# A two-layer diffusion backbone on one core: the opening of the first layer in a written-out order on all five engines

## Chip, core and metric

The kernel runs on one core of a Trainium2 chip. The time is the device time of one execution in microseconds (us). The core's engines work beside each other and wait for each other through semaphores: TensorE (PE in the profile, its weight loads PEld), VectorE (DVE), ScalarE (ACT), GpSimd (POOL), and SyncE (SP), which here only issues DMAs.

## The reference, cut to what matters

Two layers over 512 latent tokens (`x`) and 256 context tokens (`ctx`) of width 1024. The part of a layer that the change touches is its beginning: the modulation vectors, the norm, and the projection by `w_in`.

```python
mod_lat = jnp.split(jax.nn.silu(c) @ w_mod[layer] + b_mod[layer], MOD_CHUNKS, axis=-1)
mod_ctx = jnp.split(jax.nn.silu(c_ctx) @ w_mod[layer] + b_mod[layer], MOD_CHUNKS, axis=-1)
sh1, sc1, g1, sh2, sc2, g2 = [m[:, None, :] for m in mod_lat]
csh1, csc1, cg1, csh2, csc2, cg2 = mod_ctx
h_lat = rms_norm(x, attn_pre_norm[layer]) * (1 + sc1) + sh1
h_ctx = rms_norm(ctx, attn_pre_norm[layer]) * (1 + csc1) + csh1
...
(a_q, a_k, a_v, a_r, a_z, ...) = split_cols(h_lat @ w_in)
```

Behind it come three token mixers (gated linear attention, banded attention, global attention), an output projection and a gated ConvFFN, none of which the change touches.

## The kernel before

`start()` is the opening of layer 0. The 768 tokens are six tiles of 128: `tiles = (4, 5, 0, 1, 2, 3)`, the two context tiles first; I call them t0 to t5 in this order. The width of 1024 is eight k-tiles of 128 (`KT`).

- **Norm and turn of a tile.** `norm()`: ScalarE squares the tile and sums the squares (L561); `rsqrt1` makes the inverse root from the sum in five small steps (VectorE L260, ScalarE L261, VectorE L264 to L266); VectorE scales the tile by it (L563); TensorE transposes it in eight pieces into PSUM (L565), called the *turn* here; ScalarE copies k-tiles 0 to 3 and VectorE k-tiles 4 to 7 to `xt` (L566, L567).
- **Modulation.** `mod(h)`, h = 0, 1, multiplies the two vectors `c` and `c_ctx` by a half of the shift and scale columns of `w_mod`: half h serves k-tiles 4h to 4h + 3. For each half there are eight loads of 512 KB (L531), k0 to k7, and in four *pairs* of k 16 matmuls with a moving size of 512 (L535). The trace counts each fp32 matmul as two.
- **Sums and application.** `apply(h)` first adds the bias to the product (VectorE L541), turns it to columns on TensorE (L544) and writes shift and scale (L546, L547). Then, for context columns 512 to 767 and latent columns 0 to 255 and 256 to 511, and four k-tiles each: ScalarE writes the modulated value rounded to fp32r (hi, L552), VectorE scales the full value in place (L553), and VectorE, for odd k GpSimd, subtracts the two (lo, L554).
- **First projection.** `half(h, tiles)` multiplies four k-tiles of a token tile by 288 columns of `w_in` (512 to 799): 12 matmuls (L490 to L492), hi times hi, lo times hi, hi times lo. The weights are split in the same way (`weight`, L479 on ScalarE, L480 on VectorE or GpSimd). After half 1 of a tile, `rz_out` takes the result out (L696 to L699).

What sets the order: a scheduler orders the instructions of an engine by their estimated readiness, except on engines that stand in a `manual_schedule`. There they keep the order in which the code is written. In `start()` SP's order is written by hand throughout, `weave` mixing the six norms with the four pairs of `mod(0)`; TensorE's is written by hand from the first `half` on, by the table `HALF`, which puts pairs of `mod(1)` between the halves; ScalarE's and VectorE's for the second application alone. `columns()` loads four small arrays (L302 to L305), behind the second context tile in SP's program by the table entry `XF`, and turns them to columns.

Of the kernel before, what the change touches and what calls it, by code (L numbers as in the profile page):

```python
# [27 lines left out]
XF = 1  # L28
# [179 lines left out]
class Kernel:  # L208
# [90 lines left out]
    def columns(self, raw):  # L299

# [4 lines left out]
        nc.sync.dma_start(raw.f[16:32], io["ffn_pre_norm"].rearrange("l (k p) -> (l k) p", p=P))  # L305
        ps = self.mring.next()
# [159 lines left out]
    def weight(self, src, kt, w, lo="v"):  # L466
# [8 lines left out]
        else:  # L475
            nc.sync.dma_start(rv, src.rearrange("(k p) n -> p k n", p=P))
# [18 lines left out]
    def start(self, X):  # L495
# [8 lines left out]
        tring = PRing(self.PS, [(0, 2), (2, 2), (4, 2)])  # L504
        tiles = (4, 5, 0, 1, 2, 3)
        rows = F.alloc(P)
        xl = {}
        for t in tiles:
            xl[t] = xs.next().f
            nc.sync.dma_start(xl[t], self.xin(t))  # L510
            if t == tiles[XF]:
                self.columns(rows)
        sel = F.alloc(2, 2)
        idv = self.ident.rearrange("p (x j q) -> p x j q", x=2, j=2)
        nc.vector.tensor_tensor(sel.f, idv[:, 0, :, 0:2], idv[:, 1, :, 0:2], ALU.add)
# [3 lines left out]
        acc = {}  # L519
        for h in range(2):  # L520
            nc.vector.memset(ms[h].f, 0.0)
            for r in range(2):
                nc.sync.dma_start(ms[h].f[r:64:32], bm[h])

        def mod(h):

            acc[h] = ps = self.PS[:, (6 + h) * 512:(7 + h) * 512]
            for k in range(0, KT, 2):
                ws = [raw.next().f, raw.next().f]
                for x in range(2):  # L530
                    nc.sync.dma_start(ws[x], wm[h, (k + x) * P:(k + x + 1) * P])  # L531
                for x in range(2):
                    for j in range(2):
                        g = 32 * (2 * x + j)
                        nc.tensor.matmul(ps[g:g + 32, :], self.cT[:, k + x, :], ws[x][:, j], start=(k == 0), stop=(k == KT - 2), tile_position=(0, g))  # L535
                yield

        def apply(h):
# [9 lines left out]
            yield  # L548
            for r, a, b in ((1, 512, 768), (0, 0, 256), (0, 256, 512)):
                for k in range(4 * h, 4 * h + 4):  # L550
                    s, o = A[:, r, k:k + 1], B[:, r, k:k + 1]
                    nc.scalar.activation(X.r[:, 0, k, a:b], xt.f[:, k, a:b], AF.Identity, bias=o, scale=s)  # L552
                    nc.vector.tensor_scalar(xt.f[:, k, a:b], xt.f[:, k, a:b], s, o, ALU.mult, ALU.add)  # L553
                    (nc.gpsimd if k % 2 else nc.vector).tensor_tensor(X.r[:, 1, k, a:b], xt.f[:, k, a:b], X.f[:, 0, k, a:b], ALU.subtract)  # L554

        def norm():
            for t in tiles:
                x = xl[t]
# [1024 lines left out]
```

## Time and profile before

| | us |
|---|---|
| median of three runs | 1786.04 |
| lowest, highest | 1784.34, 1786.31 |
| profiled execution, device time | 1782.25 |
| its span in the trace | 1780.2 |
| TensorE busy in it | 1715.3 (96%) |
| VectorE, ScalarE, GpSimd busy | 1157.4, 794.9, 540.8 |

The opening is about the first 60 us of the span. In the page's row of 40 slices (44.5 us each) TensorE's first slice reads 7 tenths, and nearly all others 9 or 8; the DMA engines' first slice reads 9. The chain of work that ended last is TensorE's by 74%. A row of a timeline gives the start, the duration, the engine, the line and the operation, and in square brackets how long the engine had been idle and who released it.

### The profile page before, as it was taken

How to read it: one execution, taken by the hardware profiler on the slowest of the kernel's cores; microseconds unless marked ns; L12 is line 12 of the kernel's file. 1: busy time of each engine (PE TensorE's matmuls, PEld its weight loads, DVE VectorE, ACT ScalarE, POOL GpSimd, SP SyncE). 2: the span in 40 equal slices, each digit the busy share in tenths (PEclk: the TensorE clock that was granted, in tenths of full speed). 3: DMA queues.
4: the chain of work that ended last, by engine and by line, in shares of the span. 5: the costliest groups of instructions: out<-in, count | busy, mean ns of one | idle time of the engine just before them, and what ended most of it. 6: DMA issues, size and time to landing. Idle time of an engine off the chain costs nothing.

```text
span 1780.2 us, 29135 instructions
## 1 busy us (share of the span) xinstructions
PE 1715.3 (96%) x11226; PEld 1448.8 (81%) x11226; DVE 1157.4 (65%) x2356; ACT 794.9 (45%) x1652; POOL 540.8 (30%) x485
## 2 busy tenths in 40 slices
PE   7999989999899999999999999998999999999997
PEld 4898876779898888878888878878778988888886
DVE  5548986663868799774755584499764754555544
ACT  5635446773643313122221355453774653333322
POOL 2325454440420202122020262345542222222223
PEclk9999999999999999999999999999999999999999
DMA  9311134112433334353432342111105443333202
GB/s 316 92 45 37 61 101 140 58 49 94 158 117 109 112 117 153 104 182 91 152 119 71 111 144 68 49 37 49 36 1 154 149 136 95 107 95 93 73 30 89
DMA packets 169038, 177.77 MB, mean 100 GB/s; under 512 B 7382, under 2 KB 137640, under 8 KB 168644
## 3 DMA queue, kind: packets, MB, share of 16 engines
q1 hardware_dynamic: 168612, 173.56, 30.8%
q0 software_dynamic: 288, 2.36, 0.4%
q8 instruction: 88, 1.44, 0.3%
q14 instruction: 50, 0.41, 0.1%
HBM read 165.38 MB, written 10.51 MB: 99 GB/s over the span
## 4 chain that ended last, share of the span: by engine, by line
PE 74%; DVE 15%; DMA 4%; issue 4%; ACT 3%; POOL 0%; SPq 0%; DVEq 0%; ACTq 0%; POOLq 0%
PE psum L1344 28%; PE psum L490 10%; PE psum L491 10%; PE psum L492 10%; PE psum L1113 4%; PE psum L1090 3%; DMA arena_f<-in_w_mod 3%; DVE arena_f L425 2%; PE psum L1063 2%; DVE arena_r L480 2%; PE psum L1064 1%; DVE arena_f L1201 1%; DVE arena_f L1075 1%; PE psum L366 1%; PE psum L1046 1%
## 5 line engine op out<-in xcount | busy, mean ns | idle before, releaser
L1344 PE MATMUL psum<-zone_Z,arena_r 128*128 128x256 f32 (+1 forms) x2760 | 516.0, 343 | 5.2 <-DVE arena_f L1351 3.0
L1344 PEld LDWEIGHTS psum<-zone_Z,arena_r 128*128 128x128 f32 x2760 | 435.8, 189 | 74.9 <-issue 3.8
L490 PE MATMUL psum<-arena_r,zone_Z 128*128 128x256 f32 (+2 forms) x1124 | 343.9, 307 | 5.7 <-ACT arena_f L1273 3.8
L491 PE MATMUL psum<-arena_r,zone_Z 128*128 128x256 f32 (+2 forms) x1124 | 343.3, 306 | 2.7 <-POOL zone_Z L635 2.2
L492 PE MATMUL psum<-arena_r,zone_Z 128*128 128x256 f32 (+2 forms) x1124 | 342.3, 306 | 0.0
L490 PEld LDWEIGHTS psum<-arena_r,zone_Z 128*128 128x128 f32 x1124 | 213.9, 191 | 22.9 <-issue 7.6
L491 PEld LDWEIGHTS psum<-arena_r,zone_Z 128*128 128x128 f32 x1124 | 214.3, 191 | 16.6 <-issue 3.7
L492 PEld LDWEIGHTS psum<-arena_r,zone_Z 128*128 128x128 f32 x1124 | 214.0, 191 | 12.8 <-issue 4.4
L480 DVE TENSOR_TENSOR arena_r<-arena_f,arena_r 128x1024 fp32r<-128x1024 f32 (+1 forms) x111 | 157.5, 1422 | 89.7 <-ACT arena_r L479 86.2
L479 ACT CAST arena_r<-arena_f 128x1024 fp32r<-128x1024 f32 (+1 forms) x114 | 118.8, 1049 | 145.3 <-PE psum L1344 106.3
L425 DVE SCALAR_TENSOR_TENSOR arena_f<-arena_f 128x256 f32<-128x256 f32 (+1 forms) x224 | 138.9, 657 | 36.1 <-DMA arena_f<-in_w_mod 35.6
L1355 POOL TENSOR_TENSOR arena_f<-arena_f 128x768 f32<-128x768 f32 (+1 forms) x44 | 75.6, 1717 | 277.7 <-DVE arena_f L1351 250.9
L1408 DVE TENSOR_TENSOR arena_f<-arena_f,psum 128x512 f32<-128x512 f32 x100 | 68.0, 683 | 103.6 <-PE psum L492 103.5
L1334 POOL TENSOR_TENSOR arena_r<-arena_f,arena_r 128x1024 fp32r<-128x1024 f32 x22 | 53.9, 2450 | 264.3 <-ACT arena_r L1333 264.3
L1078 POOL TENSOR_SCALAR arena_f<-arena_f 128x768 f32<-128x768 f32 (+3 forms) x96 | 79.3, 829 | 89.5 <-DVE arena_f L1077 72.5
L1334 POOL TENSOR_TENSOR zone_Z<-arena_f,zone_Z 128x1024 fp32r<-128x1024 f32 x22 | 53.9, 2448 | 161.8 <-ACT zone_Z L1333 161.7
L1075 DVE TENSOR_REDUCE arena_f<-psum 128x1 f32<-128x768 f32 (+4 forms) x120 | 90.9, 766 | 14.1 <-PE psum L1064 12.1
L1349 ACT ACTIVATE arena_f<-psum,arena_f 128x512 f32<-128x512 f32 (+1 forms) x132 | 89.0, 701 | 24.1 <-PE psum L1344 24.1
L1350 DVE SCALAR_TENSOR_TENSOR arena_f<-psum,arena_f 128x511 f32<-128x511 f32 (+1 forms) x132 | 84.0, 651 | 20.0 <-ACT arena_f L1349 20.0
L1344 PE MATMUL psum<-zone_Z 128*128 128x512 f32 (+1 forms) x408 | 86.9, 366 | 0.7 <-POOL zone_Z L635 0.6
L1354 ACT ACTIVATE arena_f<-arena_f 128x768 f32<-128x768 f32 (+1 forms) x44 | 32.5, 739 | 119.1 <-DVE arena_f L1351 119.1
L1351 DVE SCALAR_TENSOR_TENSOR arena_f<-psum,arena_f 128x511 f32<-128x511 f32 (+1 forms) x132 | 84.7, 654 | 1.4
(291 smaller groups left out, 3120.2 us busy)
## 6 DMA issues: line engine op xcount, KB each, us to landing
arena_f<-in_ffn_w_up SPq DMA_DIRECT2D x88, 512.0 KB
arena_f<-in_w_mod SPq DMA_DIRECT2D x112, 256.0 KB
arena_f<-in_ffn_w_down SPq DMA_DIRECT2D x44, 512.0 KB
arena_f<-in_w_in SPq DMA_DIRECT2D x24, 512.0 KB
zone_Z<-in_w_mod SPq DMA_DIRECT2D x48, 256.0 KB
arena_f<-in_w_out SPq DMA_DIRECT2D x16, 512.0 KB
xd<-arena_f SPq DMA_DIRECT2D x16, 512.0 KB
arena_f<-xd SPq DMA_DIRECT2D x14, 512.0 KB
```

The lines of the kernel that those rows point to most:

```text
L425: nc.vector.scalar_tensor_tensor(av[:, r], x[:, i], s, av[:, r], ALU.mult, ALU.add)
L479: nc.scalar.copy(hr, rv)
L480: (nc.vector if lo == "v" else nc.gpsimd).tensor_tensor(lr, rv, hf, ALU.subtract)
L490: mm(out, lh, rh, start=first, stop=False)
L491: mm(out, ll, rh, start=False, stop=False)
L492: mm(out, lh, rl, start=False, stop=last)
L1075: nc.vector.tensor_reduce(st[:, 0:1], ps[:, 0:w], AX.X, ALU.max, negate=True)
L1334: nc.gpsimd.tensor_tensor(wp.r[:, 1], rd.f, wp.f[:, 0], ALU.subtract)
L1344: nc.tensor.matmul(p[:, po:po + n], us[s][wi][:, k], X.r[:, xi, k, o:o + n], start=(k == 0 and (wi, xi) == (0, 0)), stop=(k == KT - 1 and ...
L1349: nc.scalar.activation(d, p, AF.Identity, bias=ci[:, 3:4], scale=ci[:, 1:2])
L1350: nc.vector.scalar_tensor_tensor(d[:, 1:n], p[:, 0:n - 1], ci[:, 0:1], d[:, 1:n], ALU.mult, ALU.add)
L1351: nc.vector.scalar_tensor_tensor(d[:, 0:n - 1], p[:, 1:n], ci[:, 2:3], d[:, 0:n - 1], ALU.mult, ALU.add)
```

## The change

All of the opening is now written out in one `manual_schedule` of the five engines.

- SP: the four small arrays first (`load_columns`), then the context tiles, w_mod k0 to k3 of the first half, the first half of the `w_in` columns, k4 and k5, the bias of the first half, k6 and k7, the latent tiles, and the second half's w_mod, bias and `w_in`.
- TensorE: turn t0, a pair of `mod(0)`, turn t1, the other pairs, sums(0), half(0,t0) and half(0,t1); after these the turns of the latent tiles with the pairs of `mod(1)` and the other halves between them.
- GpSimd splits both halves of the first `w_in` columns (before: the first on VectorE) and scales the latent tiles t2 to t5 (before: VectorE). The context's lo parts are all subtracted on VectorE (`pool=False`).
- ScalarE loads the table of `Silu` with a small instruction at the very start; the PSUM banks of the norms are given by a table `NORM_BANKS`; the load of `k_rope` is held behind the last split weight's load, and the gate's loads come later.

```diff
+NORM_BANKS = 0, 2, 4, 2, 4, 4
...
-            nc.sync.dma_start(rv, src.rearrange("(k p) n -> p k n", p=P))
+            self.wdma = nc.sync.dma_start(rv, src.rearrange("(k p) n -> p k n", p=P))
...
+        def scale(t, e):
+            e.tensor_scalar(xl[t], xl[t], self.rsqrt1(nss[t], EPS * D), 0.0, ALU.mult, ALU.add)
...
+        with self.tc.manual_schedule(engines={eng.SP, eng.PE, eng.Activation, eng.DVE, eng.Pool}):
+            nc.vector.memset(one[:, 0:1], 1.0)
+            nc.scalar.activation(one[:, 1:2], one[:, 0:1], AF.Silu)
+            self.load_columns(rows)
+            load_x([t0, t1])
...
+            load_mod(0, range(0, 4))
+            load_w(0)
+            load_mod(0, range(4, 6))
+            load_bias(0)
+            load_mod(0, range(6, 8))
+            load_x([t2, t3, t4, t5])
+            m0, m1 = mod(0), mod(1)
+            self.columns(rows)
+            self.table(one[:, 0:1])
+            square(t0), scale(t0, nc.vector), square(t1), scale(t1, nc.vector)
+            turn(t0), keep(t0)
+            next(m0)
+            turn(t1), keep(t1)
+            for _ in m0:
+                pass
+            load_mod(1, range(0, 6))
+            load_bias(1)
+            load_mod(1, range(6, 8))
+            load_w(1)
+            split_w(0, nc.gpsimd)
+            square(t2)
+            sums(0)
+            apply(0, 1, 512, 768, False)
+            half(0, t0)
+            scale(t2, nc.gpsimd)
+            square(t3)
+            half(0, t1)
+            scale(t3, nc.gpsimd)
+            turn(t2), keep(t2)
+            next(m1)
+            square(t4)
+            turn(t3), keep(t3)
+            scale(t4, nc.gpsimd)
+            apply(0, 0, 0, 256)
+            square(t5)
+            half(0, t2)
+            turn(t4)
+            next(m1)
+            scale(t5, nc.gpsimd)
+            keep(t4)
+            half(0, t3)
+            turn(t5), keep(t5)
+            for _ in m1:
+                pass
+            apply(0, 0, 256, 512)
+            half(0, t4)
+            sums(1)
+            half(0, t5)
+            split_w(1, nc.gpsimd)
+            apply(1, 1, 512, 768, False)
+            apply(1, 0, 0, 256)
+            apply(1, 0, 256, 512)
+            self.vu = self.unit(io["w_in"][0], 256, 256)
+            load()
+            self.load_gate(0)
...
-            weave((norm(), 6), (mod(0), 4))
...
+        with self.tc.issue_after(self.wdma.ins):
+            nc.sync.dma_start(rope.f, io["k_rope"])
```

`square`, `scale`, `turn` and `keep` are the steps of the old `norm()`, `sums` the head of the old `apply`.

SP's queue at its beginning, before. The small rows (L302 to L305) stand behind the two context tiles, the latent tiles (L510, in_x) and all the bias loads ahead of the w_mod loads:

```order
L510 DMA arena_f<-in_ctx 128x1024 x2
L302 DMA arena_f<-in_c 8x128
L303 DMA arena_f<-in_c_ctx 8x128
L304 DMA arena_f<-in_attn_pre_norm 16x128
L305 DMA arena_f<-in_ffn_pre_norm 16x128
L510 DMA arena_f<-in_x 128x1024 x4
L523 DMA arena_f<-in_b_mod 2x512 x4
L531 DMA zone_Z_1_70<-in_w_mod 128x2x512 x6
L531 DMA arena_f<-in_w_mod 128x2x512 x2
L476 DMA arena_f<-in_w_in 128x4x288
```

and now:

```order
L301 DMA arena_f<-in_c 8x128
L302 DMA arena_f<-in_c_ctx 8x128
L303 DMA arena_f<-in_attn_pre_norm 16x128
L304 DMA arena_f<-in_ffn_pre_norm 16x128
L515 DMA arena_f<-in_ctx 128x1024 x2
L526 DMA zone_Z_1_70<-in_w_mod 128x2x512 x4
L588 DMA arena_f<-in_w_in 128x4x288
L526 DMA zone_Z_1_70<-in_w_mod 128x2x512 x2
L530 DMA arena_f<-in_b_mod 2x512 x2
L526 DMA arena_f<-in_w_mod 128x2x512 x2
L515 DMA arena_f<-in_x 128x1024 x4
L526 DMA zone_Z_1_70<-in_w_mod 128x2x512 x6
```

The small rows have moved ahead of the context tiles, the w_in half ahead of k4, and the first half's bias between k5 and k6, with the latent tiles behind.

TensorE at the beginning, before: the six turns (L565, eight transposes each) among the pairs of the first modulation (L535), then the sums (L544) and the first half:

```order
L565 MATMUL psum<-arena_f 128x128 x24
L535 MATMUL psum<-zone_Z_1_70,arena_f 32x512 x2
L565 MATMUL psum<-arena_f 128x128 x8
L535 MATMUL psum<-zone_Z_1_70,arena_f 32x512 x6
L565 MATMUL psum<-arena_f 128x128 x8
L535 MATMUL psum<-zone_Z_1_70,arena_f 32x512 x2
L565 MATMUL psum<-arena_f 128x128 x8
L535 MATMUL psum<-zone_Z_1_70,arena_f 32x512 x2
L535 MATMUL psum<-arena_f 32x512 x4
L544 MATMUL psum<-arena_f 128x4 x4
L490 MATMUL psum<-arena_r,zone_Z_2_74 128x288
```

and now the same place, up to the first half of the first tile:

```order
L574 MATMUL psum<-arena_f 128x128 x8
L539 MATMUL psum<-zone_Z_1_70,arena_f 32x512 x4
L574 MATMUL psum<-arena_f 128x128 x8
L539 MATMUL psum<-zone_Z_1_70,arena_f 32x512 x8
L539 MATMUL psum<-arena_f 32x512 x4
L548 MATMUL psum<-arena_f 128x4 x4
L493 MATMUL psum<-arena_r,zone_Z_2_74 128x288
```

Four of the six turns (L574 now) have left the place ahead of the sums. They stand behind half(0,t1), whose last matmul is the first row here, with two pairs (L539) and half(0,t2) among them:

```order
L495 MATMUL psum<-arena_r,zone_Z_2_74 128x288
L574 MATMUL psum<-arena_f 128x128 x8
L539 MATMUL psum<-zone_Z_1_70,arena_f 32x512 x4
L574 MATMUL psum<-arena_f 128x128 x8
L493 MATMUL psum<-arena_r,zone_Z_2_74 128x288
L494 MATMUL psum<-arena_r,zone_Z_2_74 128x288
L495 MATMUL psum<-arena_r,zone_Z_2_74 128x288
```

VectorE around the place where the second of these turns ends, now: the copies of t2 and t3 (L579), the inverse root of t4, and apply(0) on columns 0 to 255 (L558, L559):

```order
L579 COPY zone_Z_1_70<-psum 128x4x128 x2
L260 TENSOR_SCALAR arena_f<-arena_f 128x1
L264 TENSOR_SCALAR arena_f<-arena_f 128x1
L265 SCALAR_TENSOR_TENSOR arena_f<-arena_f 128x1
L266 SCALAR_TENSOR_TENSOR arena_f<-arena_f 128x1
L558 TENSOR_SCALAR zone_Z_1_70<-zone_Z_1_70,arena_f 128x256
L559 TENSOR_TENSOR zone_Z_2_74<-zone_Z_1_70,zone_Z_2_74 128x256
L558 TENSOR_SCALAR zone_Z_1_70<-zone_Z_1_70,arena_f 128x256 x2
L559 TENSOR_TENSOR zone_Z_2_74<-zone_Z_1_70,zone_Z_2_74 128x256
L558 TENSOR_SCALAR zone_Z_1_70<-zone_Z_1_70,arena_f 128x256
```

and the same application in the kernel before, whose rows follow the sums (L546, L547), the split of the weight and the context's part at once:

```order
L546 COPY arena_f<-psum 128x2x4
L547 SCALAR_TENSOR_TENSOR arena_f<-psum,arena_f 128x2x4
L480 TENSOR_TENSOR arena_r<-arena_f,arena_r 128x1152
L553 TENSOR_SCALAR zone_Z_1_70<-zone_Z_1_70,arena_f 128x256 x3
L554 TENSOR_TENSOR zone_Z_2_74<-zone_Z_1_70,zone_Z_2_74 128x256
L553 TENSOR_SCALAR zone_Z_1_70<-zone_Z_1_70,arena_f 128x256
L554 TENSOR_TENSOR zone_Z_2_74<-zone_Z_1_70,zone_Z_2_74 128x256
L553 TENSOR_SCALAR zone_Z_1_70<-zone_Z_1_70,arena_f 128x256 x3
L554 TENSOR_TENSOR zone_Z_2_74<-zone_Z_1_70,zone_Z_2_74 128x256
L553 TENSOR_SCALAR zone_Z_1_70<-zone_Z_1_70,arena_f 128x256
```

What was one run of applications without copies or roots between them is now cut by the copies and roots of the latent tiles.

## Rows read from the trace of the kernel before

**Rows 1.** Busy us of engines (instructions) by stretch, granted PE clock, DMA share, GB/s.

```profile
26.00:30.00 4.00, 2.24 (x17) 1.18 (x11) 1.71 (x4) 1.29 (x3) 0.00 (x0) 0.96 1.04 386
30.00:36.50 6.50, 6.50 (x28) 3.26 (x28) 6.50 (x15) 5.27 (x11) 4.01 (x4) 0.50 1.05 380
36.50:45.00 8.50, 8.50 (x63) 6.13 (x60) 3.01 (x9) 1.56 (x2) 4.25 (x3) 1.00 0.54 151
45.00:59.40 14.40, 13.69 (x99) 12.85 (x98) 12.14 (x27) 10.98 (x21) 7.04 (x7) 1.00 0.19 49
59.40:110.00 50.60, 50.56 (x379) 45.41 (x380) 17.83 (x38) 27.08 (x53) 12.59 (x14) 1.00 0.31 96
```

**Rows 2.** SyncE's DMA issues in the opening: start, duration, queue, line, operation, tiles.

```profile
0.75 0.86 SPq L510 DMA_DIRECT2D arena_f<-in_ctx  x2
1.66 0.37 SPq L302 DMA_DIRECT2D arena_f<-in_c  x1
...
2.75 0.42 SPq L305 DMA_DIRECT2D arena_f<-in_ffn_pre_norm  x1
```

**Rows 3.** ScalarE's timeline in the opening.

```profile
4.37 1.03 ACT L561 ACTIVATE psum<-arena_f 128x1024 f32<-128x1024 f32 x1 [2.03 <-DMA arena_f<-in_ctx]
...
10.62 1.28 ACT L261 ACT_TABLE_LOAD   x1
...
29.25 6.02 ACT L552 ACTIVATE zone_Z<-zone_Z,arena_f 128x256 fp32r<-128x256 f32 x12 [2.71 <-DVE arena_f L547]
...
47.02 6.03 ACT L552 ACTIVATE zone_Z<-zone_Z,arena_f 128x256 fp32r<-128x256 f32 x12 [6.03 <-DVE arena_f L547]
```

**Rows 4.** TensorE's timeline from 8 to 30 us: a turn and the last modulation matmuls of half 0.

```profile
22.15 1.09 PE L565 MATMUL psum<-arena_f 128*128 128x128 f32 x8
...
25.65 1.44 PE L535 MATMUL psum<-arena_f 128*32 128x512 f32 x6
```

**Rows 5.** TensorE's timeline from 30 to 62 us.

```profile
33.19 0.45 PE L491 MATMUL psum<-arena_r,zone_Z 128*128 128x288 f32 x1
33.43 0.44 PE L492 MATMUL psum<-arena_r,zone_Z 128*128 128x288 f32 x1
...
43.05 1.06 PE L535 MATMUL psum<-arena_f 128*32 128x512 f32 x8
...
47.05 0.30 PE L490 MATMUL psum<-arena_r,zone_Z 128*128 128x288 f32 x1
47.18 0.30 PE L491 MATMUL psum<-arena_r,zone_Z 128*128 128x288 f32 x1
...
59.44 0.39 PE L490 MATMUL psum<-arena_r,zone_Z 128*128 128x256 f32 x1 [0.39 <-DVE arena_f L699]
```

**Rows 6.** VectorE's timeline in the opening.

```profile
10.64 0.15 DVE L260 TENSOR_SCALAR arena_f<-arena_f 128x1 f32<-128x1 f32 x1 [2.12 <-ACT psum L561]
...
12.81 0.75 DVE L563 TENSOR_SCALAR arena_f<-arena_f 128x1024 f32<-128x1024 f32 x1
13.48 0.68 DVE L567 COPY zone_Z<-psum 128x512 f32<-128x512 f32 x1
...
31.70 0.82 DVE L553 TENSOR_SCALAR zone_Z<-zone_Z,arena_f 128x256 f32<-128x256 f32 x1
...
47.65 0.41 DVE L553 TENSOR_SCALAR zone_Z<-zone_Z,arena_f 128x256 f32<-128x256 f32 x1 [0.67 <-ACT zone_Z L552]
...
48.44 0.73 DVE L553 TENSOR_SCALAR zone_Z<-zone_Z,arena_f 128x256 f32<-128x256 f32 x2
```

**Rows 7.** GpSimd's timeline in the opening.

```profile
31.21 1.16 POOL L554 TENSOR_TENSOR zone_Z<-zone_Z,zone_Z 128x256 fp32r<-128x256 f32 x1 [29.90 <-DVE zone_Z L553]
```

**Rows 8.** GpSimd's groups by form over the whole span: busy, mean ns, idle before.

```profile
L1078 POOL TENSOR_SCALAR arena_f<-arena_f 128x768 f32<-128x768 f32 x36 | 36.2, 1006 | 44.3 <-DVE arena_f L1077 35.4 <-PE psum L1090 3.6 <-PE psum L1064 2.9
...
L1078 POOL TENSOR_SCALAR arena_f<-arena_f 128x256 f32<-128x256 f32 x24 | 13.6, 572 | 16.9 <-DVE arena_f L1077 15.3 <-PE psum L1064 1.6
...
L480 POOL TENSOR_TENSOR arena_r<-arena_f,arena_r 128x1152 fp32r<-128x1152 f32 x1 | 2.2, 2222 | 1.6 <-ACT arena_r L479 1.6
```

More of the change, by code (lines that the diff above doesn't have):

```diff
@@ L27 @@
 HW = 1152
-XF = 1
+NORM_BANKS = 0, 2, 4, 2, 4, 4
 TIMED = (1,)
@@ L503, in start, with load_x @@
         raw.bufs += [F.alloc(2, 512) for _ in range(NRAW)]
-        tring = PRing(self.PS, [(0, 2), (2, 2), (4, 2)])
         tiles = (4, 5, 0, 1, 2, 3)
         rows = F.alloc(P)
[L507 to L512, printed above, removed]
+        xl, nps = {}, {}
+        one = self.small.next().f
+        def load_x(ts):
+            for t in ts:
+                xl[t] = xs.next().f
+                nc.sync.dma_start(xl[t], self.xin(t))
         sel = F.alloc(2, 2)
         idv = self.ident.rearrange("p (x j q) -> p x j q", x=2, j=2)
-        nc.vector.tensor_tensor(sel.f, idv[:, 0, :, 0:2], idv[:, 1, :, 0:2], ALU.add)
         ms = [F.alloc(512), F.alloc(512)]
@@ L518, in start, with load_mod, load_bias @@
         wm = io["w_mod"][0, :, 0:2048].rearrange("a (j h n) -> h a j n", j=2, h=2)
-        acc = {}
-        for h in range(2):
-            nc.vector.memset(ms[h].f, 0.0)
+        acc, wl = {}, {}
+        def load_mod(h, ks):
+            for k in ks:
+                wl[h, k] = raw.next().f
+                nc.sync.dma_start(wl[h, k], wm[h, k * P:(k + 1) * P])
+        def load_bias(h):
             for r in range(2):
@@ new lines, in start, with square, turn @@
+        nss = {}
+        def square(t):
+            b = NORM_BANKS[tiles.index(t)]
+            nps[t] = ps = self.PS[:, b * 512:b * 512 + 1024]
+            nss[t] = self.small.next().f[:, 0:1]
+            nc.scalar.activation(ps, xl[t], AF.Square, accum_out=nss[t])
+        def scale(t, e):
+            e.tensor_scalar(xl[t], xl[t], self.rsqrt1(nss[t], EPS * D), 0.0, ALU.mult, ALU.add)
+        def turn(t):
+            for k in range(KT):
+                nc.tensor.transpose(nps[t][:, k * P:(k + 1) * P], xl[t][:, k * P:(k + 1) * P], self.ident)
@@ new lines, in start, with load_w, split_w @@
+        W = io["w_in"][0, :, 512:800]
+        wraw, hs = [], []
+        def load_w(i):
+            wraw.append(self.raw.next())
+            nc.sync.dma_start(wraw[i].f.rearrange("p (k n) -> p k n", k=4), W[i * 512:i * 512 + 512].rearrange("(k p) n -> p k n", p=P))
+        def split_w(i, e):
+            rv, pair = wraw[i].f, self.wr.next()
+            nc.scalar.copy(pair.r[:, 0], rv)
+            e.tensor_tensor(pair.r[:, 1], rv, pair.f[:, 0], ALU.subtract)
+            hs.append([shaped(pair.r[:, x], (4, 288)) for x in range(2)])
@@ L607, in start @@
+        with self.tc.manual_schedule(engines={eng.SP}):
+            for t in tiles:
+                half(1, t)
+                self.rz_out(0, t, pss[t], 0)
         for b in (raw, xt, xs, sel, rows, *ms):
```

81 lines of the change are left out of this document (23 added, 58 removed).

## The prediction

> **What bounds the kernel now.** I read the busy time of the engines by stretch first [rows 1]. From 59.4 us on TensorE is busy 50.56 of the next 50.6 us, so whatever delays the end of the opening delays everything behind it one for one, and whatever shortens the opening comes back whole. The order of the instructions behind the opening is the same in both programs on all compute engines, so the change is worth what it moves that end. Before it, TensorE computes 13.69 of 14.4 us (45.0 to 59.4) and all of 36.5 to 45; from 30 to 36.5 it is also always busy, but the granted clock is 0.50, the lower of its levels. It idles only ahead of 30 us: 1.76 of the 4 us from 26 to 30, waiting for the first modulation half and its sums.
>
> The scale of the early part is set by the loads: from 26 to 36.5 us they take all DMA engines' time at 380 GB/s [rows 1], so 512 KB cost 1.38 us. The first context tile is issued at 0.75 [rows 2] and starts its square at 4.37 [rows 3], 3.6 us later. The first half's modulation matmuls end at 25.65 + 1.44 = 27.1 [rows 4], ScalarE starts applying it at 29.25 [rows 3]: 2.2 us for the sums. The second half's last modulation matmul ends at 43.05 + 1.06 = 44.1 [rows 5], the application of that half starts at 47.02 [rows 3], and its end is the end of the opening: the first matmul of the next step starts at 59.44 [rows 5]. From 47.02 on, the chain ScalarE (hi), VectorE (scale), VectorE or GpSimd (lo) paces the rest, 12.4 us to 59.44.
>
> **The change part by part.**
>
> *Loads.* The four small rows ahead of the context tiles move those by their issue time, 1.66 to 2.75 + 0.42, 1.5 us [rows 2]: first tile at 5.8. Behind it, by bytes: second tile 7.2, w_mod rows k0 to k3 at 8.6, 9.9, 11.3, 12.7, the w_in half (590 KB, 1.55 us) 14.3, k4 and k5 to 17.0. The built order then holds k6's load behind the landing of the two bias loads, which queue behind k5; so its transfer is not in flight when k5 ends, and it pays the whole 3.6 us again: k6 at 21.0, k7 at 22.4 (without that hold 18.4 and 19.8). Latent tiles follow at 23.8 to 27.9, so square(t2) on ScalarE ends about 25. The last modulation pair ends about 23.2, **3.9 us earlier** than 27.1. That is the gain, and it is one that the first half alone has.
>
> *Sums, first context tiles.* 2.2 us for the sums give 25.4. TensorE has had little work until here (a turn and three pairs in ten us), less than in the stretch that ended at the clock of 0.50 before, so I add 0.8 for the low level: ScalarE applies from 26.2. Scaling and subtracting are both on VectorE for the context now: 48.44 - 47.65 = 0.8 us a k-tile [rows 6], four of them and ScalarE's first half microsecond make 29.9. Behind that TensorE has the last three matmuls of half(0,t0) and twelve of half(0,t1), at the low clock 0.24 us each (33.19 to 33.43 [rows 5]): 3.6, to **33.2** with the start of the first.
>
> The split of the first w_in half leaves VectorE for GpSimd (2.22 us [rows 8]); its load lands at 14.3, it is done before 20, and nothing waits for it: nothing on the path.
>
> *Latent tiles, the new place.* In the kernel before, turns t2 to t5 ran while w_mod was still arriving, ahead of 26 us, where TensorE had time; here they stand between the halves. Turn t2, a pair of the second modulation and turn t3 are 8 transposes (1.09 at 22.15 [rows 4]), 8 passes (1.06, 43.05 [rows 5]) and 8 transposes again, 3.2: 36.4. TensorE's next instruction is half(0,t2), which needs apply(0) on columns 0 to 255, and that stands on VectorE behind the copies of t2 and t3 and the inverse root of t4: copy 0.7 [rows 6], then what one inverse root takes without a table load, 12.81 - 10.64 - 1.28 = 0.9 us [rows 3, 6], then four k-tiles at 0.8, 3.2 (the odd ones' subtraction goes to GpSimd, which is slower and comes in behind: 0.4 for the last). That ends at 36.4 + 0.7 + 0.9 + 3.2 + 0.4 = 41.6. Work of TensorE in these 5.2 us: 12 matmuls of 0.13 (47.05 to 47.18 [rows 5]), 1.6. **About 3.6 us are a new wait**, where the kernel before was running matmuls.
>
> *To the end of the second modulation.* Turn t4, a pair, half(0,t3), turn t5, two pairs: 1.06 + 1.06 + 1.6 + 1.06 + 2.1 = 6.9 us at full clock, to 48.5; after a stretch in which TensorE was 1.6 of 5.2 us busy I expect the low level again, as after 26 to 30 (2.24 of 4), when 6.5 us did the work of 3.3: I add 2.0 of those 3.2, to **50.5** (44.1 before). The scaling of t4 and t5 on GpSimd costs 1.2 us each by estimate (768 columns take 1.006, 256 take 0.57 [rows 8]; 0.75 on VectorE [rows 6]): it is done beside apply(0) and half(0,t3) and I price it at nothing; without this cover turn t5 would come up to 1.2 later.
>
> *Second sums and tail.* Turn t5 ends about 48.4; copy 0.7, ScalarE's first k 0.5, then apply(0) on columns 256 to 511 with 3.2 on VectorE, the first addition of sums(1) 0.7, sums on TensorE 1.0, results 0.4: ScalarE starts apply(1) at **54.9**, against 47.02 before, 7.9 later. The tail then runs as before, with two additions: the context's two odd subtractions stay on VectorE (2 x 0.4), and GpSimd has one multiplication of the gate ahead of its last subtraction; I take 0.5 of these together, since ScalarE and TensorE overlap them. Sum: **+8.4 us**.
>
> *Nothing on the path:* the memset and the early Silu table (ScalarE waits for the first tile until 5.8 anyway; the table load of 1.28 [rows 3] leaves the chain of t1), the later k_rope and gate loads (DMA share is 0.54 and 0.19 from 36.5 [rows 1]).
>
> Bounds. Downwards: if the clock is full from 26 us on, both low-level terms and the 0.11 x 15 of the slow halves go, 4.4 us; without the hold of k6, 2 more. Upwards: GpSimd against VectorE, next but one.
>
> The profiled execution took 1782.25 with a span of 1780.2; the median of three is 1786.04. I put the difference on the median: 1786.04 + 8.4 = **1794.4**.
>
> The scaling on GpSimd could cost more than its own time. The trace shows VectorE's scaling of 256 columns at 0.41 us alone (47.65) and at 0.82 (31.70) while GpSimd runs its subtraction of 31.21 [rows 6, 7]. The Trainium skill, "SBUF — State Buffer", section "Who interferes with whom", says that an instruction of VectorE in a 2-port mode, or one with two SBUF inputs against a GpSimd instruction that reads SBUF, and one on GpSimd exclude each other for a whole instruction, the second to issue waiting. The trace agrees: the longer one has about the other's time in it. By that rule a 1.2 us scaling on GpSimd would stop apply(0) instead of running beside it: some 3 us more on the sum, where an undisturbed neighbour adds nothing; the third rival prices it from rows.
>
> **The rivals.**
>
> 1. *TensorE never waits in the new order* (faster). If the copies, roots and applications for t2 to t5 keep ahead of TensorE, the opening is TensorE's work from its first half matmul on: from 26.7, 4 turns (4.3), second modulation (4.2), sums (1.0), 144 matmuls of 0.13 (18.7) make 54.9 against 59.4 before, 4.5 less: 1781.5, and without the hold of k6 another 2 less. It decides if half(0,t2) starts within half a microsecond of turn t3 and the clock is full. Against it: half(0,t2) can't start without the copy of t3 and the application of t2, 1.6 us at the least on VectorE, and the tail of 12 us behind sums(1) isn't shorter. It would need sums(1) by 43. 11%.
>
> 2. *Waits as I say, but neither the hold of k6 nor the low clock.* 8.4 - 4.4 - 2.0 = +2.0: 1788.0. For it: the granted clock was 1.00 from 36.5 on in spite of waits of some tenths [rows 1]; bias rows are small and may slip past k5. 14%.
>
> 3. *GpSimd's scaling stops VectorE.* Scalings of t4 and t5 and the second split of 2.2 us meet applications: the first costs apply(0) most of its 1.2 us, the others together as much as one 2.2: +3 more, 1797.4. It decides if a scaling on GpSimd starts while apply(0) runs. For it the 0.82 of 31.70; against it, most of what VectorE does beside the scalings are small roots and copies out of PSUM. 14%.
>
> 4. *The delay is absorbed*, because a later load or engine sets the end of a later stage: no change. Against it 50.56 of 50.6 [rows 1]. 4%.
>
> **How the numbers follow.** Forecast 57%, 1790.5 to 1798. The range of 8 in 10 takes in rivals 2 and 3 and leaves out 1 and 4: 1787.5 to 1799.5, its upper end being the forecast's 8.4, 3 of the third rival and 2 more of low clock. About 0.2%, 3.6 us, is what a measurement of this kernel tells from no change: 1782.4 to 1789.6 is the same. Faster has most of rival 1, 9%; the same has the rest of it, rival 4 and most of rival 2, 18%; slower has the forecast, rival 3 and the upper edge of rival 2, 73%.
>
> **What would show it.** Right: the last pair of the first modulation ends near 23 and k6 lands some 3.5 us behind k5; the first half matmul comes at 26 to 27 (about 30 before); between turn t3 and the end of half(0,t2) TensorE is busy less than half of 5 us and is released by ScalarE, VectorE and GpSimd instructions of apply; the second modulation ends at 48 to 51; ScalarE starts apply(1) at 53 to 56; the first matmul of 256 columns (z done) is at 66 to 69 instead of 59.4; from there both traces run in parallel. Wrong: a second modulation that ends ahead of 45, a wait below 1 us ahead of half(0,t2), or a later stage in which the distance closes.

## The result, and the profile after

The changed kernel takes 1793.87 us (median of five runs, 1792.96 to 1798.21) against 1785.05 before (five runs, 1782.01 to 1786.31). Its ratio to the kernel before is 1.0065, with a 95% interval of 1.0052 to 1.0077: slower by 0.5 to 0.8%. The medians are 8.8 us apart and the ratio stands for 11.6, so a difference of 2 or 3 us between two versions is not settled by their medians alone. The forecast was 1794.4. The profiled execution took 1795.26 us with a span of 1793.2.

The stretches of the opening, by the same view as [rows 1]: busy us of TensorE, its weight loads, VectorE, ScalarE and GpSimd, then the granted clock, DMA share and GB/s.

```profile
26.00:30.00 4.00, 2.47 (x12) 2.12 (x12) 2.48 (x8) 2.08 (x4) 0.00 (x0) 0.75 1.04 397
30.00:36.50 6.50, 6.50 (x35) 5.49 (x34) 2.84 (x12) 2.04 (x6) 2.23 (x2) 0.63 0.89 325
36.50:45.00 8.50, 5.04 (x28) 4.24 (x25) 5.30 (x15) 5.02 (x11) 3.76 (x4) 0.80 0.78 255
...
70.00:110.00 40.00, 40.00 (x268) 35.31 (x267) 11.79 (x20) 22.43 (x37) 8.66 (x8) 1.00 0.26 82
```

From 36.5 to 45, where TensorE computed 8.50 of 8.5 us before, it computes 5.04, and the clock is below full in each of the first three stretches. From 70 us on it is busy all the time, as it was from 59.4 before.

SyncE's issues, to be read against [rows 2]:

```profile
2.37 0.89 SPq L515 DMA_DIRECT2D arena_f<-in_ctx  x2
...
8.74 1.48 SPq L530 DMA_DIRECT2D arena_f<-in_b_mod  x2
17.62 0.89 SPq L526 DMA_DIRECT2D arena_f<-in_w_mod  x2
18.55 2.11 SPq L515 DMA_DIRECT2D arena_f<-in_x  x4
```

The first context tile is issued 1.6 us later than before. The two bias loads leave SyncE at 8.74 and it stands still until 17.62, when the loads of k6 and k7 go out.

TensorE, from the wait for k6 to the first matmul of the next step, against [rows 4, 5]:

```profile
21.64 3.15 PE L539 MATMUL psum<-arena_f 128*32 128x512 f32 x8 [2.92 <-DMA arena_f<-in_w_mod]
25.59 1.05 PE L548 MATMUL psum<-arena_f 128*128 128x4 f32 x8 [0.80 <-DVE arena_f L545]
27.67 0.40 PE L493 MATMUL psum<-arena_r,zone_Z 128*128 128x288 f32 x1 [1.02 <-ACT zone_Z L557]
...
36.60 1.09 PE L574 MATMUL psum<-arena_f 128*128 128x128 f32 x8
39.26 0.40 PE L493 MATMUL psum<-arena_r,zone_Z 128*128 128x288 f32 x1 [1.57 <-ACT zone_Z L557]
40.99 0.40 PE L494 MATMUL psum<-arena_r,zone_Z 128*128 128x288 f32 x1 [1.32 <-DVE zone_Z L559]
...
42.21 0.61 PE L494 MATMUL psum<-arena_r,zone_Z 128*128 128x288 f32 x1 [0.57 <-POOL zone_Z L559]
...
50.18 1.04 PE L539 MATMUL psum<-arena_f 128*32 128x512 f32 x8
```

```profile
68.44 0.40 PE L494 MATMUL psum<-arena_r,zone_Z 128*128 128x288 f32 x1 [1.03 <-POOL zone_Z L559]
...
69.07 0.28 PE L493 MATMUL psum<-arena_r,zone_Z 128*128 128x256 f32 x1
```

The first half's last pair runs from 21.64 to 24.79 (27.1 before), 2.92 us of wait in front of it. Turn t3 ends at 37.69. Behind it come three waits, for the first hi part (ScalarE), for the first lo part (VectorE) and for one of GpSimd's: 3.5 us in all, where before TensorE was always busy. The second modulation ends at 51.2 (44.1 before), the next step starts at 69.07 (59.44 before).

What TensorE waits for there, on VectorE and GpSimd, and ScalarE's start of the second application (47.02 before):

```profile
39.27 0.41 DVE L558 TENSOR_SCALAR zone_Z<-zone_Z,arena_f 128x256 f32<-128x256 f32 x1
39.71 1.22 DVE L559 TENSOR_TENSOR zone_Z<-zone_Z,zone_Z 128x256 fp32r<-128x256 f32 x1
```

```profile
39.51 1.15 POOL L570 TENSOR_SCALAR arena_f<-arena_f 128x1024 f32<-128x1024 f32 x1 [4.94 <-ACT zone_Z L557]
41.34 0.82 POOL L559 TENSOR_TENSOR zone_Z<-zone_Z,zone_Z 128x256 fp32r<-128x256 f32 x1 [0.68 <-DVE zone_Z L558]
...
65.31 1.41 POOL L758 TENSOR_TENSOR arena_f<-arena_f 128x256 f32<-128x256 f32 x1 [0.93 <-ACT arena_f L756]
66.68 1.70 POOL L559 TENSOR_TENSOR zone_Z<-zone_Z,zone_Z 128x256 fp32r<-128x256 f32 x1
```

```profile
55.44 6.02 ACT L557 ACTIVATE zone_Z<-zone_Z,arena_f 128x256 fp32r<-128x256 f32 x12 [2.72 <-DVE arena_f L551]
```

Along the trace the same instruction comes 9.6 us later than before at 69 us, and at the end of the span 13.0; the profiled execution of the kernel before took 1782.25, below its median. The largest step behind the opening is near 1375 us, where the distance grows by some 2 us: TensorE waits about as long there as the kernel before (3.2 and 3.0 us), but the granted clock from 1365 to 1380 us is 0.77, against 1.00 in the kernel before.

### The profile page after: what moved, and what is told of

Read it like the earlier page. It is cut to its first block, busy times and chain, and to the rows that moved or that the text cites. A ratio compares the mean times of both kernels' runs of the same rounds, so it can differ in the third digit from the quotient of the medians.

```text
span 1793.2 us, 29131 instructions
## 1 busy us (share of the span) xinstructions
PE 1721.3 (96%) x11226; PEld 1454.6 (81%) x11226; DVE 1153.5 (64%) x2356; ACT 793.0 (44%) x1652; POOL 543.7 (30%) x486
## 4 chain that ended last, share of the span: by engine, by line
PE 73%; DVE 16%; DMA 4%; issue 3%; ACT 3%; POOL 1%; SPq 0%; DVEq 0%; ACTq 0%; POOLq 0%
PE psum L1405 27%; PE psum L493 10%; PE psum L494 10%; PE psum L495 10%; PE psum L1174 3%; PE psum L1151 3%; DMA arena_f<-in_w_mod 3%; DVE arena_f L428 2%; PE psum L1124 2%; DVE arena_r L483 1%; PE psum L1125 1%; DVE arena_f L1262 1%; PE psum L369 1%; DVE arena_f L992 1%; DVE arena_f L1136 1%
## 5 line engine op out<-in xcount | busy, mean ns | idle before, releaser
L493 PEld LDWEIGHTS psum<-arena_r,zone_Z 128*128 128x128 f32 x1124 | 217.0, 193 | 23.3 <-issue 5.3
L494 PEld LDWEIGHTS psum<-arena_r,zone_Z 128*128 128x128 f32 x1124 | 217.3, 193 | 19.8 <-issue 3.7
L495 PEld LDWEIGHTS psum<-arena_r,zone_Z 128*128 128x128 f32 x1124 | 217.1, 193 | 12.7 <-issue 4.2
```

Source lines behind the costliest of these rows:

```text
L493: mm(out, lh, rh, start=first, stop=False)
L494: mm(out, ll, rh, start=False, stop=False)
L495: mm(out, lh, rl, start=False, stop=last)
```

## The experiments

The measure of the opening is the start of the first matmul of 256 columns (59.44 before, 69.07 in the changed kernel), which one trace gives to about 1 us: how long the low clock lasts behind the new wait differs (turn t4 and the pair behind it, first matmul at 44.30, take 1.41 and 1.06 us in the changed kernel, and 1.91 and 1.60 in a run below that differs only by transposes at its very start). Times are medians, with the ratio to the kernel before. Where a run adds transposes of the identity, their results are used nowhere.

### The hold of k6

```diff
-            load_mod(0, range(4, 6))
+            load_mod(0, range(4, 8))
             load_bias(0)
-            load_mod(0, range(6, 8))
```

> The changed kernel with the first half's two bias loads issued behind the w_mod loads k6 and k7 instead of ahead of them. Theory (the fixed order makes everything behind the first modulation half a chain of waits, and the hold of k6 is one link of it): TensorE's wait of 2.9 us ahead of the k6 pair goes to under 1 us, the first modulation half ends at 22 to 23 instead of 24.8, and the first matmul of 256 columns comes 1.5 to 2.5 us earlier than 69.07, so 66.5 to 67.6; time 1.5 to 2.5 us below the changed kernel, still 6 to 8 above the kernel before. Rival (the start is not a link, later waits set the end): first half earlier, but the 256-column matmul still at 68.5 to 69.5.

TensorE's timeline: the first of the late pairs, the sums, and the next step.

```profile
18.67 1.05 PE L539 MATMUL psum<-arena_f 128*32 128x512 f32 x4 [0.30 <-DMA arena_f<-in_w_mod]
...
23.30 1.87 PE L548 MATMUL psum<-arena_f 128*128 128x4 f32 x8 [2.27 <-DVE arena_f L545]
```

```profile
67.41 0.28 PE L493 MATMUL psum<-arena_r,zone_Z 128*128 128x256 f32 x1
```

The k6 matmuls start 3 us earlier and wait 0.30 instead of 2.92. The bias itself is now late: the sums wait 2.27 us, so that they start at 23.30 instead of 25.59. 1.66 us of the gain reach the end; the time is 1792.15 (ratio 1.0042, 1.0028 to 1.0057). The hold is a link of the chain.

### Work for the new wait

```diff
             turn(t3), keep(t3)
+            next(m1)
+            next(m1)
             scale(t4, nc.gpsimd)
...
             turn(t4)
-            next(m1)
```

> The changed kernel with the second and third pair of the second modulation moved into TensorE's wait behind turn t3 (ahead of the first projection of t2), instead of behind turns t4 and t5. Theory (the wait of 3.6 us ahead of and in half(0,t2) is empty time that other work could fill): TensorE's idle between turn t3 and the end of half(0,t2) falls by about 2.1 us, the second modulation ends 2 us earlier than 51.2, and the 256-column matmul comes at 66.5 to 67.5 instead of 69.07; with a higher granted clock behind it another 0.5 to 1. Rival (the end hangs on VectorE's and GpSimd's chain of copies, roots and applications, not on TensorE): no gain, 68.5 to 69.5.

```profile
37.72 1.93 PE L539 MATMUL psum<-zone_Z,arena_f 128*32 128x512 f32 x16
...
41.08 0.40 PE L494 MATMUL psum<-arena_r,zone_Z 128*128 128x288 f32 x1 [1.11 <-DVE zone_Z L559]
```

```profile
67.46 0.28 PE L493 MATMUL psum<-arena_r,zone_Z 128*128 128x256 f32 x1
```

Two pairs fit into 1.93 us of the wait, and the end is 1.6 us earlier. TensorE's idle time between turn t3 and the end of half(0,t2) falls by 1.4 us, from 3.46 to 2.04, less than the 2.1 expected; the time is 1792.51 (1.0042, 1.0027 to 1.0056). The second modulation ends at 48.6, 2.6 earlier, but the second sums still stand behind half(0,t4), which waits for VectorE and GpSimd three times: the end hangs on both, as the theory had it for TensorE and the rival for the chain.

### The engine that scales

`scale(t2)` to `scale(t5)` with `nc.vector` for `nc.gpsimd`.

> The changed kernel with the scaling of t2 to t5 on VectorE (0.75 us) instead of GpSimd (1.1). Theory (the place of the turns is the cost, not the engine): the 256-column matmul within 0.8 us of 69.07, either way. Rival (GpSimd's scaling stops VectorE): the subtraction that took 1.22 us at 39.71 takes 0.43 or 0.84, and the end comes 1.5 to 3 us earlier.

VectorE's timeline at the same place, and the end:

```profile
40.17 0.75 DVE L570 TENSOR_SCALAR arena_f<-arena_f 128x1024 f32<-128x1024 f32 x1
...
41.28 0.42 DVE L559 TENSOR_TENSOR zone_Z<-zone_Z,zone_Z 128x256 fp32r<-128x256 f32 x1
```

```profile
69.88 0.28 PE L493 MATMUL psum<-arena_r,zone_Z 128*128 128x256 f32 x1
```

The subtraction is back at 0.42 (1.22 beside GpSimd's scaling), but the scaling of 0.75 us now stands in VectorE's own queue in front of it. The end is 0.8 later, the time 1794.5 (1.0059, 1.0037 to 1.0080). GpSimd's scaling does stop VectorE; moving it back wins nothing.

### The low clock

```diff
             turn(t1), keep(t1)
-            for _ in m0:
-                pass
+            next(m0)
+            warm(7, 4)
+            next(m0)
+            warm(7, 20)
+            next(m0)
+            warm(7, 5)
```

and so around the first halves of t0 and t2; `warm(b, n)` is n transposes of the identity into bank b, 64 in all.

> The changed kernel with 60 transposes of the identity into unused PSUM columns put into TensorE's waits (between the first half's pairs, around the sums, and ahead of and in the first projections of t0 and t2); their results are not used. It measures what the low clock costs. Theory: the granted clock from 14 to 45 us goes from 0.63 to 0.86 to 0.9 or more, the last matmuls of half(0,t0) and half(0,t1) take 0.13 instead of 0.24 us each, and the 256-column matmul comes 1.5 to 3.5 us earlier than 69.07 (I had put 4.4 us in all on the clock). Rival (the clock falls only while other engines are waited for, and costs nothing): 68.5 or later.

```profile
26.00:30.00 4.00, 3.55 (x21) 2.63 (x21) 3.13 (x10) 2.08 (x4) 0.00 (x0) 1.00 1.03 392
30.00:36.50 6.50, 6.37 (x49) 4.98 (x49) 2.80 (x12) 3.95 (x10) 2.23 (x2) 1.00 0.87 319
36.50:45.00 8.50, 7.31 (x52) 5.51 (x52) 5.20 (x14) 3.70 (x8) 3.83 (x4) 1.00 0.77 253
```

```profile
66.09 0.28 PE L493 MATMUL psum<-arena_r,zone_Z 128*128 128x256 f32 x1
```

The granted clock is 1.00 throughout, and the end comes 3.0 us earlier: that is what the low clock costs in the opening, net of the time that the transposes take themselves. The time is 1792.03 (1.0043, 1.0028 to 1.0058). By the medians that is 1.8 below the changed kernel, by the ratios 3.9, and in the two traces 2.9 at the end of the span; the runs do not show whether less than the 3.0 came through.

### The small rows

```diff
-            self.load_columns(rows)
             load_x([t0, t1])
+            self.load_columns(rows)
```

> The changed kernel with the four small rows loaded behind the two context tiles instead of ahead of them. Theory (the loads set the first half's end, and the rows hold all of them back by 1.5 us): first context tile 1.3 to 1.6 us earlier, first modulation half 0.8 to 1.6 earlier than 24.8, 256-column matmul at 67.5 to 68.4. Rival (the columns, which the modulation needs, come later and eat it): 68.8 or later.

```profile
6.65 0.31 PE L310 MATMUL psum<-arena_f 48*128 48x48 f32 x1 [6.65 <-DMA arena_f<-in_ffn_pre_norm]
12.30 1.94 PE L574 MATMUL psum<-arena_f 128*128 128x128 f32 x8 [5.33 <-DVE arena_f L260]
...
21.14 1.05 PE L539 MATMUL psum<-arena_f 128*32 128x512 f32 x4 [1.10 <-DMA arena_f<-in_w_mod]
23.18 1.05 PE L539 MATMUL psum<-arena_f 128*32 128x512 f32 x4 [0.98 <-DMA arena_f<-in_w_mod]
```

```profile
3.21 2.92 SPq L526 DMA_DIRECT2D zone_Z<-in_w_mod  x4
...
17.27 0.89 SPq L526 DMA_DIRECT2D arena_f<-in_w_mod  x2
```

```profile
68.72 0.28 PE L493 MATMUL psum<-arena_r,zone_Z 128*128 128x256 f32 x1
```

The theory's range was missed. The matmul of the columns stands ahead of turn t0 on TensorE; it now waits for the rows until 6.65 (3.64 in the changed kernel), the copy and table behind it hold ScalarE, and the first turn starts at 12.30 instead of 9.30. The rival took these late columns for the cause, but they do not hold the first half: TensorE still waits 1.10 and 0.98 us for the loads of k6 and k7. The rows stand ahead of the w_mod loads in both orders, so the first of these leaves SyncE at 3.21 instead of 3.30, and k6, still behind the bias, at 17.27 instead of 17.62; why the transfers gain no more from the earlier tiles is not shown. The k7 matmuls end 0.6 us earlier, turn t3 1.2 earlier (36.50), and the end 0.35 earlier; in between the granted clock is 0.64 from 36.5 to 45 us, 0.80 in the changed kernel. The time is 1792.59 (1.0043, 1.0027 to 1.0059).

### The three links together

The bias ahead of all w_mod loads (in its own run it stood behind k7), two pairs in the wait, and 38 transposes instead of 64 in the others.

> The changed kernel with its turns where it has them, and the three single edits together: the first half's bias ahead of the w_mod loads, two pairs of the second modulation in the wait behind turn t3, identity transposes in the other waits. Singly they brought the 256-column matmul from 69.07 to 67.41, 67.46 and 66.09. Theory (three separate links of one chain): they add up to 6 to 7.5 us, 61.5 to 63.5; what is left above 59.44 are the four turns (4.3 us) and the longer chain of VectorE behind them. Rival (they are the same microseconds counted three times): 65.5 or later.

```profile
63.51 0.28 PE L493 MATMUL psum<-arena_r,zone_Z 128*128 128x256 f32 x1
```

5.6 us earlier, of 6.2 that the three brought singly and a little less than the 6 expected at the least. The edits are not quite the single ones, but most of the gains add up: they are in the main separate links. 4.1 us are left above the kernel before. The time, 1791.57 (1.0035, 1.0021 to 1.0049), is only 2.3 below the changed kernel's.

### The turns in their old place

Latent tiles and bias ahead of the w_mod loads; then, on all engines still by hand:

```diff
+            turn(t0), keep(t0)
+            square(t2), scale(t2, nc.gpsimd)
+            turn(t1), keep(t1)
...
+            turn(t4), keep(t4)
+            next(m0)
+            turn(t5), keep(t5)
+            next(m0)
+            next(m0)
...
+            sums(0)
+            apply(0, 1, 512, 768, False)
+            apply(0, 0, 0, 256)
+            apply(0, 0, 256, 512)
+            half(0, t0)
+            next(m1)
+            half(0, t1), half(0, t2)
```

> The changed kernel, still in a written-out order on all five engines, with the latent tiles back in the place that they had: loaded ahead of the w_mod loads (the bias with them, w_in behind k7), squared, scaled on GpSimd, turned and copied ahead of the end of the first modulation; the halves and the pairs of the second modulation in the order of the kernel before. Theory (the place of the turns is the cost): the first modulation ends at 25 to 27, later than 24.8, but TensorE has no wait over 1 us ahead of half(0,t2), and the first matmul of 256 columns comes at 58.5 to 61, against 69.07 in the changed kernel and 59.44 before; time within 2 us of the kernel before. Rival (a fixed order on all engines costs by itself, wherever the turns stand): 64 or later, and 5 us or more above the kernel before.

```profile
60.13 0.38 PE L493 MATMUL psum<-arena_r,zone_Z 128*128 128x256 f32 x1 [0.92 <-DVE arena_f L752]
```

8.9 of the 9.6 us are gone, though the first half ends at 25.0 instead of 24.8 and the order is still fixed: a fixed order costs nothing by itself here, the place of the turns does. Loads, applications and pairs moved with the turns, so the 8.9 belong to the arrangement as a whole. The time is 1788.16 (1.0022, 1.0012 to 1.0031), 5.7 below the changed kernel and 3.7 above the kernel before, where 0.7 to 2 were expected. In this build the scheduler's order behind the opening differs from that of the two kernels, on TensorE at four places (near 264, 1070, 1080 and 1085 us). In the traces the distance to the kernel before grows by 1.7 us at the first of them; the run with two pairs in the wait has the other three. I did not separate this from other causes.

### Pairs directly behind halves, with and without transposes

> As the run with the turns in their old place, with three more edits: the second half's bias is loaded with the first's and its k6 and k7 directly behind k5; each pair of the second modulation stands directly behind one half, so that the second sums come ahead of the halves of the last two tiles; and 17 transposes of the identity fill TensorE's waits around the first sums. Theory (the end of the opening is the second sums plus a tail of about 12.4 us, and the low clock costs 2 to 3 us ahead of it): second modulation ends at 38.5 to 41 instead of 44.1, the application of the second half starts at 41 to 43.5 instead of 47.02, and the 256-column matmul comes at 54 to 57; time 2.5 to 5 us below the kernel before. Rival (the last loads of the second modulation or TensorE's own work bind): 58 or later, no faster than the kernel before.

> The run with the turns in their old place, the second bias early and one pair behind each half, without the 17 transposes. In the run with them the 256-column matmul came at 58.04 (59.44 before), but its time was 6 us above the kernel before. Theory (the end of the opening comes through one for one, and the transposes or something that they shift made the loss): 256-column matmul at 58.5 to 60.5, time within 2 us of the kernel before. Rival (the loss comes with the early end of the opening or the early loads, not with the transposes): same opening, time 4 us or more above the kernel before.

The starts of the next step, with 17 transposes and without:

```profile
58.04 0.28 PE L493 MATMUL psum<-arena_r,zone_Z 128*128 128x256 f32 x1
```

```profile
59.77 0.28 PE L493 MATMUL psum<-arena_r,zone_Z 128*128 128x256 f32 x1
```

With transposes the opening ends 1.4 us earlier than before, at 58.04 where 54 to 57 were expected, and the time is 1790.42 (1.0025, 1.0011 to 1.0039), not 2.5 to 5 us faster but some 6 slower. Without them the opening ends 0.3 later and the time is 1783.63 (0.9993, 0.9984 to 1.0002), that of the kernel before. The transposes' 1.7 us of opening cost 6.8 us in the end. Behind the opening the two have the same order of instructions on the compute engines.

### Transposes where TensorE idles anyway

```diff
             self.columns(rows)
+            warm(7, 20)
             self.table(one[:, 0:1])
```

in the changed kernel (the first control), and in the run without transposes of the last section (the second).

> A control: the changed kernel with 20 transposes of the identity on TensorE at its very start, where it idles for 5 us; nothing else differs, and the order of all engines behind is the same. The kernels with added transposes ended the opening early but lost 4 to 12 us again between 660 and 1100 us of their trace, where TensorE waits for VectorE and VectorE for late w_mod loads. Theory (the end of the opening comes through, the losses behind have nothing to do with the added instructions): 256-column matmul at 68 to 69.5, time within 1.5 us of the changed kernel. Rival (added instructions at the start cost something later, as by a shifted stream of instructions): same opening, time 3 us or more above the changed kernel.

> The same run without transposes, with the control's 20 transposes of the identity at the very start, where TensorE idles; the order behind is the same. The control cost the changed kernel 4.4 us. Theory (added TensorE instructions cost some us in later stages, whatever the opening): 256-column matmul within 0.8 us of 59.77, time 3 to 6 us above 1783.63. Rival (the control's loss belongs to the changed kernel): time within 1.5 us of 1783.63.

```profile
4.88 4.53 PE L565 MATMUL psum<-arena_f 128*128 128x128 f32 x20 [0.85 <-ACT arena_f L313]
```

```profile
69.92 0.28 PE L493 MATMUL psum<-arena_r,zone_Z 128*128 128x256 f32 x1
```

```profile
58.12 0.38 PE L493 MATMUL psum<-arena_r,zone_Z 128*128 128x256 f32 x1 [0.87 <-DVE arena_f L766]
```

The transposes fill 4.5 us in which TensorE had nothing to do. The runs came out as the first control's rival and the second's theory had them. In the changed kernel the opening ends 0.85 later and the time is 1798.23 (1.0081, 1.0067 to 1.0094), 4.4 above the changed kernel (2.9 by the ratios, whose intervals overlap). In the other the opening ends 1.65 earlier and the time is 1788.38 (1.0030, 1.0016 to 1.0043), 4.8 above the same kernel without them. So both control runs show a loss that lies behind the opening, 3.5 and 6.4 us by the medians; it is clear of the noise in the second. What makes it is open.

In some of these traces TensorE waits more between 600 and 1110 us: it is busy 499.92 us there in the changed kernel, 493.33 with the transposes of the clock run and 496.64 in the first control, and the added waits are for VectorE. But runs without any transposes show some of this too, 497.82 with the two pairs and 497.73 with the small rows behind the context tiles. The second control's trace shows 499.81 and no such place; it is the fastest of that run's six executions (1784.04, the others 1786.52 to 1792.27), so it hardly holds the loss.

### A pair ahead of the first half

```diff
+            next(m1)
             half(0, t0)
-            next(m1)
             half(0, t1)
```

> The run without transposes, with one edit: the first pair of the second modulation stands ahead of half(0,t0), in TensorE's wait of 2.5 us for the first application, instead of behind that half. It adds no instruction. Theory (that wait is empty, and the end of the opening comes through when nothing is added): 256-column matmul 0.5 to 1.5 us earlier than 59.77, time 0.5 to 1.5 us below that run's 1783.63. Rival (the pair's loads land too late, or later waits take it back): 59.5 or later, time 1784 or more.

```profile
27.16 2.17 PE L539 MATMUL psum<-zone_Z,arena_f 128*32 128x512 f32 x8
```

```profile
56.48 0.38 PE L493 MATMUL psum<-arena_r,zone_Z 128*128 128x256 f32 x1 [0.87 <-DVE arena_f L751]
```

The opening ends 3.3 us earlier than without the edit, more than expected, and 3.0 earlier than in the kernel before. The pair does not only use the wait: the granted clock is 1.00 from 26 to 36.5 us, where the run without the edit shows 0.85 and then 0.57. The time is 1783.16 (0.9993, 0.9984 to 1.0002): the median 1.4 below the kernel before, not to be told from it. No version here beats the kernel before beyond its interval.

## Why the prediction was right, point by point

**The frame.** The time was to follow the end of the opening one for one. For the change it did as far as the times can tell: the next step starts 9.6 us later, the median is 8.8 above, and the ratio stands for 11.6 (9.3 to 13.7). It also held, to 1.2 us of medians, in the runs of the bias, the pairs, the scaling, the clock, the rows and the pairs behind halves without transposes, whose openings ended 0.3 to 10.4 us later than before. It did not hold in the other four runs with added transposes, which lost 3 to 7 us behind the opening, nor to 1.2 us in the run with the turns in their old place (0.7 became 3.7), and the last run's 3.0 us came through as 1.4.

**Loads.** k6 was to land at 21.0 behind the hold, and its matmuls start at 21.64. The first half was to end at 23.2 and ended at 24.8. Two things were missed: k7 came 0.6 us later than its place by bytes (22.4), and its matmuls ran at the low level (23.00 to 24.79 in the first control, where they have a row of their own), for which I had no term. The 1.5 us for the early rows was right as a delay of the context tiles' issue (1.6), but wrong as a delay of all loads behind them: with the rows in their old place k6's load leaves 0.35 us earlier, the first half ends 0.6 earlier, and 0.35 come back at the end.

**Sums and context.** 2.2 us for the sums: 24.79 to 27.02. The 0.8 us that I added here for the low clock is not there: the sums' matmuls (25.59) take 1.05 us, as they did before. This makes up for half of the late first half. The halves of t0 and t1 end at 34.46 instead of 33.2, nearly all of it the later start (27.67 for 26.7); with their low clock they took what I had put.

**The new wait** is the main term. 3.6 us of wait were forecast and 3.5 measured, released by ScalarE, VectorE and GpSimd in that order. VectorE's copy of t3 and the inverse root of t4 take 1.6 us, as forecast: turn t3 ends at 37.69, the first multiplication of apply(0) starts at 39.27. The stretch from turn t3 to the end of half(0,t2) is longer than forecast, 6.6 against 5.2 us, mostly because the clock falls in it: from 42.2 on the matmuls start 0.24 us apart, which was 0.13 with the clock at its upper level; I had put this low stretch behind it. Both together, to the end of the second modulation, were 14.1 us from turn t3's forecast end at 36.4 and measured 13.5 from 37.7: right as a sum.

**The tail** was mis-sized. I put 0.5 us on it; it is 13.6 us against 12.4, 1.2 more. GpSimd's gate multiplication at 65.31 takes 1.41 ahead of its last subtraction, which takes 1.70 beside VectorE's weight split and releases TensorE at 68.44. The subtraction itself is no longer than in the kernel before, where it ran beside the split too, but it starts 11.2 us behind ScalarE's first instruction of the application instead of 9.5:

```profile
56.56 1.65 POOL L554 TENSOR_TENSOR zone_Z<-zone_Z,zone_Z 128x256 fp32r<-128x256 f32 x1 [0.69 <-DVE zone_Z L553]
```

I had the multiplication as overlapped; nothing is left there that could cover it.

**The rivals.** The first (TensorE never waits) falls with 3.5 us of wait. The second (no hold, full clock) falls with 2.92 us ahead of k6 and a granted clock of 0.75, 0.63 and 0.80 in the three stretches; its prices were 2.0 (2.6 by the landing times of the prediction itself) and 4.4, and the runs gave 1.66, net of a late bias, and 3.0. The third (GpSimd stops VectorE) is there as a mechanism: the subtraction took 1.22 us beside a scaling of 1.15 that had started 0.2 earlier. The Trainium skill, "SBUF — State Buffer", section "Who interferes with whom", has the second of the two wait for the whole of the first. By that rule the subtraction would take the 0.95 that were left of GpSimd's scaling and its own 0.43, 1.38; the row has 1.22, near it and not quite. The pair of rows that the prediction read the same way, VectorE's 0.82 at 31.70, has less than the rule too: of GpSimd's 1.16 from 31.21 there were 0.67 left, which makes 1.08 with VectorE's own 0.41. It cost 0.8 us at one place, not 3: the scaling at 31.99 met only small steps of a root on VectorE, those at 33.46 and 43.94 met nothing there. The fourth (absorbed) is excluded by 8.8 us.

**The sum.** Along the chain the forecast was early by 1.6 us at the end of the first half, 1.3 at turn t3, 0.7 at the end of the second modulation, 0.5 at the second application and 1.2 at the next step (67.8 for 69.07). The errors partly cancel: too little for k7 and for the tail, too much for the low clock behind the wait. That the median came within 0.5 us of the forecast is closer than the steps were.

## What to carry to other kernels

Ahead of a fixed order, write down for each engine what the next instruction waits for: work that fills a load's shadow in one place (four turns ahead of the modulation's end) becomes path and wait when it stands in a chain of four engines. An early end of one stage, here the first modulation half, is worth nothing if the next stage is given new work to wait for. Transposes that keep a clock up are to be measured in the whole program's time: here they gave 3.0 us where they stood, 1.8 of it by the medians, and in three other runs the whole time was 4 to 7 us longer with them than without. Work of the kernel's own in such a wait, a pair of the second modulation, kept the clock at 1.00 as well and added nothing.

## What the runs showed that I had not expected

Twenty added transposes on TensorE at its start, where it had 5 us to spare, cost 4.4 and 4.8 us of the whole time in two kernels by the medians; 17 around the first sums cost 6.8 with an opening that ended 1.7 us earlier. The order of all other instructions on the compute engines was the same in each pair. The granted clock over the span is lower with the transposes, if only a little (medians 0.983 for 0.985, 0.986 for 0.988 and 0.987 for 0.988), and whether that is a cause or comes of the waits is not shown. Where the time is lost is not settled: waits for VectorE between 600 and 1110 us are there in several traces, also in some without transposes.

A wait that is only a little longer can cost more than itself through the clock. Near 1365 us of the kernel without transposes TensorE waits 3.1 us for ScalarE and the clock stays at 1.00 behind it; in the run with 17 transposes it waits 4.2 us at the same place, the granted clock from 1365 to 1380 us is 0.77, and the distance between the two traces grows by 3.2 us.

A clock of 1.00 in the whole opening was worth 3.0 us of opening. Four small rows moved ahead of two tiles of 512 KB held the tiles' issue by 1.6 us, but the first w_mod load, which stood behind the rows in either order, by only 0.1.
